# Four blocks of a small transformer: the 31-tap convolution as matmuls, attention's reciprocals as small ones, and layer 0's inverse directly behind its matrices

## The chip, the cores and the metric

The kernel runs on one core of a Trainium2 chip. The core has five engines with queues of their own: TensorE (PE) for matmuls, VectorE (DVE), ScalarE (ACT), GpSimd (POOL), and SyncE (SP), which issues most of the DMAs. PE reads its operands from SBUF and writes into PSUM, eight banks of 128x512 floats; DVE and ACT read the banks. The metric is the device time of one execution in microseconds (us), the median of several runs.

## The reference

The input is a sequence of 256 tokens of 1024 features with a context of as many. `reference` runs two blocks of one kind (layers 0 and 1) and then two of another (the second blocks). Layer 0:

```python
def even_mixer(u_lat, u_ctx, need_ctx, w_in, w_out, conv_w, a_log, dt_bias, out_norm,
               q_norm, w_q_up, kv_norm, w_kv_up, rope):
...
    o_lat, o_ctx = gdn_bidirectional(gdn_prepare(lat[0], lat[2], lat[3], conv_w, a_log, dt_bias),
                                     gdn_prepare(ctx[0], ctx[2], ctx[3], conv_w, a_log, dt_bias))
...
    b_lat = blocked_attention(q_l, jnp.concatenate([k_c, k_l], 1), jnp.concatenate([v_c, v_l], 1), scale)
    y_lat = jnp.concatenate([a_lat, b_lat.reshape(b, s_len, -1)], -1) @ w_out
```

`gdn_bidirectional` is a gated delta rule in chunks of 64 tokens, forwards and backwards. Per chunk and head it builds a lower triangular matrix from the keys, inverts it, and uses the inverse in a scan over the chunks; q, k and v come through a convolution of 5 taps and a silu, q and k also through a norm. Layer 1 has a neighbourhood attention (8 heads) and a grouped one (8 heads on 2 key heads). The two second blocks have an attention in which each token sees the 64 keys that a small index network picks, a pooling, and a causal convolution of 31 taps, each of 256 channels with taps of its own:

```python
def conformer_conv(u, conv_dw, conv_b, ln_g, ln_b, conv_pw):
    a, g = jnp.split(u, 2, axis=-1)
    y = a * jax.nn.sigmoid(g)
    y = lax.conv_general_dilated(
        y, conv_dw[:, None, :], window_strides=(1,), padding=[(CONV_KERNEL - 1, 0)],
        dimension_numbers=('NWC', 'WIO', 'NWC'), feature_group_count=CONV_WIDTH)
    y = y + conv_b
    y = jax.nn.silu(layernorm(y, ln_g, ln_b))
    return jnp.einsum('bsc,cd->bsd', y, conv_pw)
```

Each mixer ends in a linear of its output, and each block in a feed-forward network. Every number is a 32-bit float.

## The kernel before

**Linears.** A weight is loaded from memory in pieces (`wraw`) and split into a high part, cast on ACT (L270, `whi`), and a low part, a subtraction mostly on DVE (L272, `wlo`). Three matmuls (L549 to L551) then stand for one. L306 and L307 split activations in the same way. A matmul of plain floats, such as a transposition (with the identity `const_id`), is one instruction of the program and two in the trace.

**The order of the work.** The source gives each engine its instructions in the order of the calls; a scheduler that runs when the kernel is built then moves them within what their data and buffers allow. So the order on an engine is fixed before the run, and an instruction that waits holds up all that stand behind it on that engine. Buffers set much of it. PSUM banks are handed out by kind (`bank(K, "tp")`), each kind with a number of banks: in layer 0 `g` 3, `s` 2, `tp`, `po`, `gv` one each (`acc` is `s`, `aux` is `g`); in the mixers of layer 1 and of the second blocks `acc` 2, `s` 2, `tp` 2, `aux` and `po` one each (`gv` is `aux`).

**Layer 0** (`l0_mixer`). `gdn_conv` does, for the key, query and value columns, the linear (in `s`) and then the 5 taps: ACT multiplies the identity by a tap, which gives a diagonal 128x128 matrix (L882), and PE multiplies the shifted input by it and sums in a bank (L886). `gdn_norm` normalizes (L941 to L945). `gdn_matrices` transposes (L1028) and forms the products of keys with keys and of queries with keys (L1040), the second kind in its second call; `gdn_blocks` sends the triangular matrices out to memory and back in another layout; `gdn_invert` inverts blocks of 32 on DVE (31 steps of L1086 and L1088), sends them out and back again (`scx`), and finishes on DVE (L1105) and PE (L1115, L1128). `gdn_run` is the scan (from L1154), followed by latent attention (`l0_mla`), four pairs of heads. In the source, the inverse's call comes after the query and value convolutions, the gate's linear and the second matrices. The modulation of layer 0 (`mod_chunk`) multiplies two columns by a weight of 1024x512 for each of its chunks (L372), and brings the rows to columns (L378 for the two gate chunks 4 and 5).

**Attention** (`attend` in layers 0 and 1, `s_attend` in the second blocks). For two heads the scores come in two banks; DVE finds the maximum, ACT takes the exponential and its sum (`sm`), PE transposes the result (L674, L1653), ACT and DVE copy it, and PE multiplies it by the values into `po` (L685, L1659). The sums: DVE takes the reciprocal of a sum that it reads 64 times over (L693), a matmul with the identity turns it (L695) into a bank `rb`, and `attended` multiplies the output by it. In layer 1, `na` is the neighbourhood's attention for a block of 128 tokens, `gqa` the grouped one, and the list `late` holds transposes of the grouped one's keys and queries (L1345).

**The second blocks' mixer** (`s_mixer`). It runs the index network and `choose`, which picks keys on DVE (L1605 to L1621), linears, rotations (`qkv`), and then

```python
        qkv()
        conv(1)
        conv(0)
        choose(0)
        pool_out(0)
        pool_out(1)
        finish()
        att(1)
        att(0)
```

`conv` multiplies the shifted input by a tap on ACT (L1516) and adds it on POOL (L1517), 30 times for each half of the channels. `finish` transposes the sum (L1531), and does the layer norm, the silu (L1543 on) and the product with the pointwise weight (L1553).

## Time and profile before

| | |
|---|---|
| three runs, us | 2169.08, 2181.03, 2183.77 (median 2181.03) |
| the profiled execution, us | 2178.34 |
| its span from first to last instruction, us | 2176.6 |
| its mean granted PE clock | 0.917 |
| PE, DVE, ACT, POOL busy, us | 1992.6, 1382.2, 931.8, 370.7 |

The granted clock is the share of PE's full speed that the chip gave it in a stretch. The times of the rows are of the profiled execution, counted from its first instruction.

### The profile page before, as it was taken

The numbers are of one execution on the slowest core, as the hardware profiler recorded it, in microseconds if no ns is written. First come the engines' busy times: TensorE is split into PE (matmuls) and PEld (weight loads), VectorE is DVE, ScalarE is ACT, GpSimd is POOL, SyncE is SP. The second block draws the span as 40 slices with busy tenths as digits, with TensorE's granted clock in tenths as the row PEclk, the third lists the DMA queues.
The fourth block names the chain that finished last, engine by engine and source line by source line (L and its number), as shares of the span: only waits on it lengthen the run. The fifth ranks groups of instructions, "written<-read, shape, count | busy, mean of one in ns | idle before, by whom it ended". The sixth has DMA issues, their size and how long they took to land.

```text
span 2176.6 us, 30043 instructions
## 1 busy us (share of the span) xinstructions
PE 1992.6 (92%) x11008; PEld 1585.0 (73%) x11008; DVE 1382.2 (64%) x2699; ACT 931.8 (43%) x1612; POOL 370.7 (17%) x454
## 2 busy tenths in 40 slices
PE   6989799898999999899879998988899998879998
PEld 4778578678878778676557887865688787558886
DVE  5665557767776744638575555785765568666644
ACT  4533443344222234444454443753554357345532
POOL 2211112301000000213130002641200057040000
PEclk9999799899999999999788999966999999579999
DMA  8344540233676632223044573513556443055652
GB/s 279 90 112 122 190 131 26 67 98 111 191 259 215 189 106 93 90 68 97 20 145 141 164 230 100 145 54 113 168 175 195 153 113 109 29 164 166 191 186 68
DMA packets 186947, 291.82 MB, mean 134 GB/s; under 512 B 28472, under 2 KB 75704, under 8 KB 186800
## 3 DMA queue, kind: packets, MB, share of 16 engines
q1 hardware_dynamic: 172720, 272.54, 40.2%
q0 software_dynamic: 5472, 16.13, 2.3%
q10 hardware_dynamic: 8608, 1.23, 0.4%
q8 instruction: 87, 1.43, 0.3%
q14 instruction: 60, 0.49, 0.1%
HBM read 281.44 MB, written 8.41 MB: 133 GB/s over the span
## 4 chain that ended last, share of the span: by engine, by line
PE 75%; DVE 13%; DMA 5%; ACT 4%; issue 2%; POOL 1%; SPq 0%; ACTq 0%; DVEq 0%; POOLq 0%
PE acc L549 17%; PE acc L550 17%; PE acc L551 17%; DVE wlo L272 2%; DMA wraw<-in_w_in_dram 2%; PE s L549 2%; PE s L550 2%; PE s L551 2%; PE po L685 2%; PE tp L886 2%; DMA wraw<-in_w_mod_dram 1%; PE gv L372 1%; ACT whi L270 1%; PE tp L674 1%; PE s L1642 1%
## 5 line engine op out<-in xcount | busy, mean ns | idle before, releaser
L272 DVE TENSOR_TENSOR wlo<-wraw,whi 128x512 fp32r<-128x512 f32 (+4 forms) x748 | 488.7, 697 | 292.4 <-ACT whi L270 276.5
L270 ACT CAST whi<-wraw 128x1024 fp32r<-128x1024 f32 (+4 forms) x420 | 413.4, 989 | 456.1 <-PE acc L551 180.9
L549 PE MATMUL acc<-whi,u 128*128 128x512 f32 (+3 forms) x1320 | 512.5, 391 | 28.3 <-ACT u L306 15.9
L550 PE MATMUL acc<-wlo,u 128*128 128x512 f32 (+3 forms) x1320 | 511.7, 389 | 4.4 <-DVE wlo L272 4.4
L551 PE MATMUL acc<-whi,u 128*128 128x512 f32 (+3 forms) x1320 | 510.3, 388 | 0.8 <-DVE u L307 0.7
L549 PEld LDWEIGHTS acc<-whi,u 128*128 128x128 f32 x1320 | 254.3, 193 | 80.9 <-ACT u L306 18.2
L550 PEld LDWEIGHTS acc<-wlo,u 128*128 128x128 f32 x1320 | 254.3, 193 | 55.2 <-DVE wlo L272 8.0
L551 PEld LDWEIGHTS acc<-whi,u 128*128 128x128 f32 x1320 | 253.2, 192 | 52.3 <-DVE u L307 4.3
L272 POOL TENSOR_TENSOR wlo<-wraw,whi 128x512 fp32r<-128x512 f32 (+1 forms) x92 | 115.1, 1280 | 400.5 <-ACT whi L270 400.4
L549 PE MATMUL acc<-u,whi 128*128 128x512 f32 (+1 forms) x480 | 174.1, 369 | 5.0 <-ACT u L1558 2.7
L550 PE MATMUL acc<-u,whi 128*128 128x512 f32 (+1 forms) x480 | 174.0, 364 | 2.4 <-DVE u L307 2.4
L551 PE MATMUL acc<-u,wlo 128*128 128x512 f32 (+1 forms) x480 | 173.1, 365 | 2.2 <-DVE wlo L272 2.2
L1517 POOL TENSOR_TENSOR u<-u,cvm 128x256 f32<-128x256 f32 x120 | 100.3, 836 | 64.2 <-ACT cvm L1516 55.8
L549 PEld LDWEIGHTS acc<-u,whi 128*128 128x128 f32 x480 | 93.9, 197 | 21.6 <-ACT u L1558 3.1
L431 DVE SCALAR_TENSOR_TENSOR msum<-mraw,u,msum 128x512 f32<-128x512 f32 x140 | 100.8, 746 | 13.4 <-DMA mraw<-in_w_mod_dram 12.4
L550 PEld LDWEIGHTS acc<-u,whi 128*128 128x128 f32 x480 | 94.5, 197 | 17.7 <-DVE u L307 3.1
L551 PEld LDWEIGHTS acc<-u,wlo 128*128 128x128 f32 x480 | 94.1, 197 | 17.6 <-DVE wlo L272 2.8
L307 DVE TENSOR_TENSOR u<-aux,u 128x512 fp32r<-128x512 f32 (+2 forms) x92 | 56.8, 629 | 34.8 <-ACT u L306 34.4
L306 ACT CAST u<-aux 128x512 fp32r<-128x512 f32 (+2 forms) x92 | 48.5, 541 | 59.2 <-PE aux L724 25.9
L549 PE MATMUL acc<-whi,dxh 128*128 128x512 f32 x176 | 69.7, 396 | 1.9 <-ACT dxh L306 1.9
L550 PE MATMUL acc<-wlo,dxh 128*128 128x512 f32 x176 | 69.6, 395 | 0.0
L551 PE MATMUL acc<-whi,dxl 128*128 128x512 f32 x176 | 69.0, 396 | 0.0
(501 smaller groups left out, 3037.8 us busy)
## 6 DMA issues: line engine op xcount, KB each, us to landing
wraw<-in_w_up_dram SPq DMA_DIRECT2D x64, 512.0 KB, 3.9
wraw<-in_w_down_dram SPq DMA_DIRECT2D x64, 512.0 KB, 4.2
...
```

The source lines that it names most:

```text
L270: self.K.nc.scalar.copy(hi, raw)
L272: e.tensor_tensor(lo[:, k], raw[:, k], hi.bitcast(F32)[:, k], op=ALU.subtract)
L306: (hi_eng or nc.scalar.copy)(hi, src)
L307: nc.vector.tensor_tensor(lo, src, hi.bitcast(F32), op=ALU.subtract)
L372: nc.tensor.matmul(ps[32 * j:32 * j + 32, :], K.cl[:, g + k, :], raw[:, k, :], start=(g + k < 4), stop=(g + k >= 4))
L431: nc.vector.scalar_tensor_tensor(accs[s], raw[:, k, :], c, accs[s], op0=ALU.mult, op1=ALU.add)
L549: mm(ps, ah, bh, start=start, stop=False)
L550: mm(ps, ah, bl, start=False, stop=False)
L551: mm(ps, al, bh, start=False, stop=stop)
L685: nc.tensor.matmul(po[hh * 64:hh * 64 + 64, c:c + 128], v(hh, j), pts[hh][0][:, j * 128:(j + 1) * 128], start=(j == 0), stop=(j == nj - 1))
L886: nc.tensor.matmul(tp[:, t * 128:(t + 1) * 128], x[:, t // 2, t % 2 * 128 + j:t % 2 * 128 + j + 128], dg[j], start=(j == 0), stop=(j == 4))
L1517: nc.gpsimd.tensor_tensor(o, o, m, op=ALU.add)
```

## The change

1. The second blocks' convolution goes to PE. `taps` makes a diagonal matrix per tap on ACT, and one of the bias as a 32nd tap on an input of ones; `conv` sums 2 x 32 products for each half of the tokens in a bank, `po` for one and `tp` for the other. The result stands by tokens, so that L1531's transposes go. `finish` reads the banks.
2. The sums' reciprocal is taken once, of 2 (or 4) columns, into a tile `R`; at a block's end `normed` spreads it over 512 columns (a copy on DVE), turns it with four matmuls (L700 of the new file) into `aux` (in layer 0 `gv`), and multiplies.
3. The two heads of a pair take score banks of one kind: in layer 1, odd pairs of the grouped attention and of the second block of `na` take `acc`, even ones `s`; in the second blocks head group 1 takes `acc`. Layer 1's `late` runs before `na(1)`.
4. In layer 0 `gdn_invert` is called directly behind `gdn_blocks`, and the query's norm and matrices ahead of the value's convolution and the gate. The second matrices' products go to the banks `gv` and `po` instead of two of kind `g`. Modulation chunks 6 to 9 come before the latent attention, and the gate chunks 4 and 5 within it, before its third pair, with the bias in a tile of its own.

```diff
@@ attend @@
-    sums_row(K, sm.unsqueeze(1), rb, c)
+    nc.vector.reciprocal(R[:, x], sm)
+    c = 128 * x
...
+def inverse_sums(K):
+    return cut(K, [128, 4, 2], F32, "rs", 2)
+
+def normed(K, y, po, R, kind):
+
+    rb = bank(K, kind)
+    w = cut(K, [128, 512], F32, "pt", K.np)
+    K.nc.vector.tensor_copy(w.rearrange("p (x d) -> p x d", d=64), bc(R.rearrange("p x h -> p (x h)"), [128, 8, 64], 2))
+    for x in range(4):
+        K.nc.tensor.matmul(rb[:, x * 128:x * 128 + 128], w[:, x * 128:x * 128 + 128], K.ident,
                            start=True, stop=True)
+    K.nc.scalar.copy(y, rb)
+    K.nc.vector.tensor_tensor(y, po, y, op=ALU.mult)
@@ l0_mla @@
+        if pair == 2:
+            gates()
@@ gdn_matrices @@
-        kk = [aux(K), aux(K)]
+        kk = [bank(K, "gv"), bank(K, "po")] if second else [aux(K), aux(K)]
@@ layer 1 @@
-                   ("s", "acc", "tp", "acc") if t == 1 and pair >= 1 else ("s", "s", "tp", "tp"))
+                   ("acc", "acc", "tp", "tp") if t == 1 and pair % 2 else ("s", "s", "tp", "tp"))
...
-    na(1)
     for f in late:
         f()
+    na(1)
@@ s_conv @@
-    def conv(c):
-        o = cv[:, c, :]
-        nc.scalar.activation(o, yp[:, c, 0:256], AF.Identity, scale=dw[:, i, c, 0:1], bias=dwb[:, i, c:c + 1])
-        na = 31 if c == 0 else 31
-        for j in range(1, na):
-            m = cut(K, [128, 256], F32, "cvm", 2)
-            nc.scalar.mul(m, yp[:, c, j:j + 256], dw[:, i, c, j:j + 1])
-            nc.gpsimd.tensor_tensor(o, o, m, op=ALU.add)
...
+    def taps(c):
+
+        for j in range(32):
+            if j % 3 == 0:
+                dg = cut(K, [128, 3, 128], F32, "dg", 2)
+            nc.scalar.mul(dg[:, j % 3, :], K.ident, dw[:, i, c, j:j + 1] if j < 31 else dwb[:, i, c:c + 1])
+            yield j, dg[:, j % 3, :]
+
+    def conv():
+
+        ps = [bank(K, "po"), bank(K, "tp")]
+        for c in range(2):
+            for j, dg in taps(c):
+                for t in range(2):
+                    nc.tensor.matmul(ps[t][:, c * 128:c * 128 + 128],
+                                     yp[:, c, t * 128 + j:t * 128 + j + 128] if j < 31 else ones, dg,
+                                     start=(j == 0), stop=(j == 31))
+        return ps
@@ s_attend @@
-    pss = [bank(K, "s") for _ in range(2)]
+    pss = [bank(K, "acc" if g else "s") for _ in range(2)]
@@ s_mixer @@
-        conv(1)
-        conv(0)
+        cv = conv()
         choose(0)
         pool_out(0)
         pool_out(1)
-        finish()
+        finish(cv)
@@ l0_mixer @@
-                        LX = gdn_blocks(K, Om)
+                        gdn_invert(K, *gdn_blocks(K, Om))
                     with Pool(K, "gq"):
                         with On(K, pg):
                             gdn_conv(K, W, 0, 4, True, True)
+                        gdn_norm(K, 0)
+                        gdn_matrices(K, True)
+                        with On(K, pg):
                             gdn_conv(K, W, 8, 4, False, True)
                             gdn_gate(K, W)
-                        gdn_norm(K, 0)
-                        gdn_matrices(K, True)
...
-                with On(K, g2):
-                    gdn_invert(K, *LX)
...
-                        for n in range(4, 10):
-                            mod_chunk(K, W, K.po, 0, n)
-                        l0_mla(K, Om)
+                        for n in range(6, 10):
+                            mod_chunk(K, W, K.cur, 0, n)
+                        l0_mla(K, Om, lambda: [mod_chunk(K, W, K.cur, 0, n) for n in (4, 5)])
```

PE in layer 0, before: behind the gate's last linear matmul come the second matrices (keys `u_138`, queries `u_137`) and the inverse.

```order
L886 MATMUL tp_1544<-cvo_1537,u_439 128x128 x4
L886 MATMUL tp_1544<-cdg_1538,u_439 128x128
...
L551 MATMUL s_1692<-whi_1590,u_149 128x512
L1028 MATMUL tp_1755<-const_id_75,u_138 128x128 x4
L378 MATMUL gv_3235<-mrow_3233,const_id_75 2x512
L1028 MATMUL tp_1762<-const_id_75,u_137 128x128 x4
L1040 MATMUL g_1769<-gT_1767,gT_1760 64x64
...
L1115 MATMUL g_2013<-b_2009,u_144 32x32 x32
L1128 MATMUL g_2083<-u_144,b_2010 32x32 x32
```

The same in the new order (L892 is L886 before, L1034 is L1028, L1046 is L1040, L1121 is L1115, L1134 is L1128, L1160 is L1154): the second matrices and the inverse stand directly behind the linear of the values' last chunk (`s_2083`), and ahead of the values' products and of the gate.

```order
L551 MATMUL s_2083<-u_148,wlo_1907 128x512
L1034 MATMUL tp_1715<-const_id_75,u_137 128x128 x4
L1046 MATMUL gv_1722<-gT_1720,gT_1713 64x64
L1046 MATMUL po_1723<-gT_1720,gT_1713 64x64
...
L1121 MATMUL g_1136<-b_1132,u_144 32x32
L1134 MATMUL g_1206<-u_144,b_1133 32x32 x32
...
L1046 MATMUL po_1855<-gT_1852,gT_1845 64x64
L892 MATMUL tp_1945<-cvo_1938,u_436 128x128 x4
L892 MATMUL tp_1945<-cdg_1939,u_436 128x128
...
L1160 MATMUL g_2313<-u_139,u_143 64x64
```

Behind it the values' products and the gate's linear alternate, and the scan's first matmuls (L1160) stand among the gate's.

PE in the first second-block mixer, in the new order: the last wide linear matmul (`acc_12546`), then the taps (L1533) among the index network's products (`s_12829`) and the transposes of queries and keys (L1351, before L1345).

```order
L551 MATMUL acc_12546<-whi_12514,u_9658 128x384
L1533 MATMUL tp_12613<-dg_12624,u_11691 128x128
L1533 MATMUL po_12612<-dg_12624,u_11691 128x128
L1533 MATMUL tp_12613<-dg_12624,u_11691 128x128
...
L1533 MATMUL tp_12613<-dg_12634,u_11691 128x128
L549 MATMUL s_12829<-u_12035,u_12064 128x128
...
L1351 MATMUL aux_12588<-const_id_75,akd_12578 128x128 x2
L549 MATMUL s_12840<-u_12035,u_12071 128x128
L1533 MATMUL po_12612<-dg_12644,u_11691 128x128
```

Of the layer's 128 taps 11 stand ahead of these rows. Its last ones, the transposes of the layer norm (L1552, before L1543), attention's products with the values (L1668, before L1659) and the scores behind them (L1647):

```order
L1533 MATMUL po_12612<-dg_12821,u_11696 128x128
L1533 MATMUL tp_12613<-dg_12821,u_11696 128x128
L1552 MATMUL acc_12953<-const_id_75,lnx_12975 128x128 x2
L1668 MATMUL po_13003<-pt_13027,u_11685 64x256
L1668 MATMUL po_13003<-pt_13039,u_11685 64x256
...
L1647 LDWEIGHTS u_11656
L1647 MATMUL acc_13054<-u_11689,u_11656 128x256
```

The product into `po_13003` stands behind the last tap, since there is one bank `po`.

## Rows read from the trace of the kernel before

**Rows 1.** The page of the kernel before, its parts 1, 4 and 5: busy time of each engine (PEld is PE's weight loads) with its share of the span and its instructions, the shares of the chain of waits by engine, and the group of the convolution's adds (both layers, busy us and mean ns of one).

```profile
PE 1992.6 (92%) x11008; PEld 1585.0 (73%) x11008; DVE 1382.2 (64%) x2699; ACT 931.8 (43%) x1612; POOL 370.7 (17%) x454
...
PE 75%; DVE 13%; DMA 5%; ACT 4%; issue 2%; POOL 1%; SPq 0%; ACTq 0%; DVEq 0%; POOLq 0%
...
L1517 POOL TENSOR_TENSOR u<-u,cvm 128x256 f32<-128x256 f32 x120 | 100.3, 836 | 64.2 <-ACT cvm L1516 55.8
```

**Rows 2.** The windows by stage. Columns: from and to, length, then busy us and instructions of PE, of its weight loads, of DVE, ACT and POOL, then the granted clock of PE (1.00 is full), the busy share of the DMA engines and GB/s.

```profile
204.00:276.00 72.00, 58.93 (x885) 41.81 (x883) 33.79 (x113) 29.28 (x62) 13.11 (x30) 0.75 0.51 170
276.00:384.00 108.00, 105.02 (x1139) 82.09 (x1139) 71.96 (x125) 43.08 (x100) 21.58 (x30) 1.00 0.26 79
1018.00:1138.00 120.00, 98.30 (x537) 67.60 (x537) 79.55 (x148) 53.51 (x106) 30.82 (x30) 0.81 0.23 71
1342.00:1436.00 94.00, 78.29 (x490) 72.26 (x489) 71.91 (x136) 64.70 (x135) 60.93 (x76) 0.94 0.46 130
1436.00:1502.50 66.50, 54.63 (x200) 34.97 (x200) 41.87 (x122) 22.16 (x65) 5.80 (x8) 0.50 0.09 28
1851.00:1919.00 68.00, 55.02 (x201) 35.20 (x201) 43.61 (x124) 21.19 (x64) 5.67 (x8) 0.50 0.09 27
```

**Rows 3.** Three lines of the kernel in the view of one line by shape, all calls of the span: min, median and max ns of one, first and last start. L1516 is the convolution's multiplication, L882 makes a diagonal matrix for layer 0's short convolution, L693 is the reciprocal of the sums.

```profile
L1516 ACT ACTIVATE cvm<-u,u x120: 494/507/550, 1363.5 to 1860.1; 128x256 f32<-128x256 f32 x120
...
L882 ACT ACTIVATE cvo<-const_id,u x32: 385/388/403, 88.9 to 183.6; 128x128 f32<-128x128 f32 x32
...
L693 DVE RECIPROCAL rs<-sm x32: 935/953/954, 311.9 to 1099.8; 128x128 f32<-128x128 f32 x32
L693 DVE RECIPROCAL rs<-asm x8: 1695/1743/1753, 1456.9 to 1908.6; 128x256 f32<-128x256 f32 x8
```

**Rows 4.** PE's time line in layer 0, from the products of the short convolution (L886) to the first linear matmul behind them: start, us, instruction, count.

```profile
137.99 1.91 PE L886 MATMUL tp<-cvo,u 128*128 128x128 f32 x8
139.70 0.64 PE L886 MATMUL tp<-cdg,u 128*128 128x128 f32 x2
...
141.40 1.06 PE L886 MATMUL tp<-cvo,u 128*128 128x128 f32 x8
...
148.12 1.05 PE L886 MATMUL tp<-cvo,u 128*128 128x128 f32 x8
...
152.50 0.47 PE L549 MATMUL s<-u,whi 128*128 128x512 f32 x1
```

**Rows 5.** The windows of two stretches of 6 us around the end of the first second-block mixer's linear work; columns as in rows 2.

```profile
1430.00:1436.00 6.00, 1.98 (x18) 1.58 (x16) 5.83 (x16) 3.88 (x9) 4.56 (x6) 0.84 0.00 1
1460.00:1466.00 6.00, 6.00 (x23) 3.64 (x22) 3.07 (x11) 0.91 (x4) 0.00 (x0) 0.50 0.00 0
```

**Rows 6.** DVE's subtraction that makes the low part of a weight (L272): in 1342–1436 us at 128x384 (from the groups of DVE by shape), and on the page over the whole span, mostly at 128x512.

```profile
L272 DVE TENSOR_TENSOR wlo<-wraw,whi 128x384 fp32r<-128x384 f32 x16 | 12.7, 852 | 0.7 <-ACT whi L270 0.7
...
L272 DVE TENSOR_TENSOR wlo<-wraw,whi 128x512 fp32r<-128x512 f32 (+4 forms) x748 | 488.7, 697 | 292.4 <-ACT whi L270 276.5
```

**Rows 7.** Two pieces of the chain of waits in the first second-block mixer: start, us, what.

```profile
1428.40 0.96 DVE u L1605
...
1490.51 3.38 DVE rs L693 x2
```

**Rows 8.** DVE's time line in layer 0: the first and the last step of the inverse's loop, the norm's multiplication, and the first step that uses what came back from memory. In brackets the idle time before, and what ended it.

```profile
142.94 0.27 DVE L1086 TENSOR_TENSOR b<-gL,u 128x62 f32<-128x62 f32 x1 [13.65 <-DMA gL<-scr]
...
186.03 2.99 DVE L945 TENSOR_TENSOR u<-u,rsy 128x512 f32<-128x512 f32 x2
...
191.43 0.22 DVE L1088 TENSOR_TENSOR u<-u,b 128x62 f32<-128x62 f32 x1
...
199.56 1.23 DVE L1105 STREAM_TRANSPOSE b<-u 32x1024 f32<-32x1024 f32 x1 [3.29 <-DMA u<-scx]
```

**Rows 9.** PE's time line in layer 0: a chunk of linear work behind the last query product and the next product; then a wait for a modulation weight, the first matmuls of the inverse on PE and the first of the scan.

```profile
162.56 0.48 PE L549 MATMUL s<-u,whi 128*128 128x512 f32 x1
...
168.25 1.05 PE L886 MATMUL tp<-cvo,u 128*128 128x128 f32 x8
...
232.80 1.92 PE L372 MATMUL gv<-wraw,u 128*32 128x512 f32 x4 [4.63 <-DMA wraw<-in_w_mod_dram]
...
240.02 1.20 PE L1115 MATMUL g<-b,u 32*32 32x32 f32 x64
...
262.33 0.33 PE L1154 MATMUL g<-u,u 64*64 64x64 f32 x2 [0.27 <-ACT u L1132]
```

**Rows 10.** The windows of the last part of layer 0's stretch ahead of the scan, and of the scan's first operands; columns as in rows 2.

```profile
246.00:262.00 16.00, 15.46 (x402) 9.98 (x394) 14.44 (x67) 9.83 (x26) 5.33 (x21) 0.57 0.64 207
262.00:276.00 14.00, 13.36 (x117) 11.72 (x114) 7.65 (x24) 5.73 (x12) 0.00 (x0) 0.55 0.25 87
```

**Rows 11.** Layer 1's attention: two windows, columns as in rows 2, and of PE's time line the first and the last of the five lone transposes there that follow a wait.

```profile
1024.00:1048.00 24.00, 19.54 (x103) 12.97 (x103) 19.05 (x49) 11.24 (x25) 9.98 (x12) 0.72 0.11 36
1048.00:1078.00 30.00, 23.78 (x97) 14.61 (x96) 12.70 (x21) 9.37 (x22) 0.00 (x0) 0.60 0.07 20
...
1050.24 0.44 PE L1345 MATMUL aux<-const_id,lkd 128*128 128x128 f32 x2 [0.53 <-ACT pt L713]
...
1056.37 1.09 PE L1345 MATMUL aux<-const_id,lx 128*128 128x128 f32 x4 [1.01 <-DVE u L307]
```

74 lines of the change are left out of this document (29 added, 45 removed).

## The prediction

> **What bounds the kernel now.** I read the page first, then the windows by stage, then TensorE's (PE's) time line where a window shows idle time or a low clock, and the chain of waits for the two places where the chain leaves PE. The page shows PE busy for 92% of the span, and 75% of the chain on it [rows 1]. So a change pays in only two ways: it fills time in which PE idles, or it brings PE's granted clock back to its upper level (1.00 is 2.4 GHz, 0.50 is 1.2 GHz). The windows show where either is to be had [rows 2]. In 204–276 us (layer 0, between the V convolution and the scan) PE idles 13 of 72 us at a mean clock of 0.75; in 1018–1138 (layer 1's attention) 22 of 120 at 0.81; in 1436–1502.5 (the end of the first second-block mixer) 12 of 66.5 at 0.50, and the same again in 1851–1919. In 276–384 the clock is 1.00 and 105 of 108 us are busy: there nothing is to be had. The change touches just the stretches with slack; outside them I expect no difference.
>
> The sum is made against the profiled execution, 2178.3 us. It lies 2.7 us under the median of the three runs, 2181.0, whose own spread is 15 us. The bound of 1% used for the chances is 22 us: faster is below 2159, slower above 2203.
>
> **1. The convolution of the two second-block mixers.** What goes is 120 adds on GpSimd (POOL), 0.836 us each, 100.3 us [rows 1], with their 120 ScalarE (ACT) multiplications of 0.507 us. What comes, per layer, is 64 diagonal matrices on ACT (31 taps and the bias, two channel halves) and 128 matmuls on PE, which the trace counts as 256, since each full-float one is two instructions. Layer 0's short convolution has the same two operations. ACT makes a 128x128 diagonal in 0.388 us [rows 3], so 24.8 us a layer in place of 60 x 0.507 = 30.4. On PE, 40 instructions take from 148.12 to 152.50 = 4.38 us at the upper clock, 0.110 each; at the lower, eight take 1.71 us (137.99 to 139.70), 0.214 each [rows 4]. So a layer's convolution costs PE **28.0 us at 2.4 GHz and 54.7 us at 1.2 GHz**.
>
> Does that fit into what PE leaves idle? In the order of the change only 11 of the 128 matmuls come early. The rest stand after the last wide linear matmul, between the query and key transposes and the scores, where before PE waits for VectorE (DVE). That linear work ends at about 1432 us: in 1430–1436 PE is busy 2.0 of 6 us at a clock of 0.84, and from there on it is 0.50, even in 1460–1466, where PE is busy all the time [rows 5]. From 1436 to the end PE does 54.6 us of work at 0.50 [rows 2], that is 27 us at 1.00 if all of it scales; I take 30. With the convolution in the gap I expect the clock to stay up: eight of its kind take 1.91 us at 137.99 and 1.06 at 141.40, so it rises within a run of them, and at 148.12 it is up [rows 4]. Then 28 + 30 = 58 us of PE work follow.
>
> The start moves too. While POOL adds, DVE's steps are long: L272 on 128x384 takes 852 ns, more than the 697 ns mean of a group that is mostly 128x512 [rows 6]; by elements it should take 0.52. That is 5 us on these 16 alone, and DVE is on the chain there (1428.40) [rows 7]. Of perhaps 10 us that DVE gets back, I take half for the linear work's end, 1427, since not each of these steps has PE waiting behind it. The Trainium skill (SBUF — State Buffer, "SBUF: two separate sides") says that DVE and GpSimd share a port pair as an exclusive lock, where a DVE step with two SBUF inputs blocks for the whole GpSimd instruction. The trace agrees in kind, with 0.33 us per L272 step, less than half an add. By that rule up to half of a layer's 50 us of adds, 25 us, would come back to DVE.
>
> To 1427 + 58 = 1485 I add 12 us of waits: ACT's diagonals, of which few buffers are open, and the end, where the layer norm waits for the last tap and attention's products wait for the banks that the convolution holds. Before, PE waits about as much from 1436 on. The end is then near 1497 against 1502.5, **5.5 us a layer, 11 in both**. The bounds: all 12 us of waits hidden and 10 us from DVE, 22 a layer; clock at 0.50 throughout, 1427 + 54.7 + 54.6 + 12 = 1548, a loss of 46 a layer.
>
> **2. The sums' reciprocals.** 32 reciprocals of 0.953 us and 8 of 1.743 go, 44.4 us of DVE [rows 3]. 40 on 2 or 4 columns come, which I price by DVE's shortest kind of row, 0.22 us [rows 8], 8.8 in all, and 12 copies of 128x512 (0.70 by [rows 6]), 8.4. DVE loses 27 us, but almost nowhere on the chain, where PE covers it. In the mixers' ends two of 1.74 stand on the chain, 3.38 us at 1490.51 [rows 7]; I have put that in the 12 us above. Elsewhere: 0, hidden by PE; uncovered, 0.95 per score pair.
>
> **3. Layer 0.** DVE's triangular inverse already runs at 142.94–191.65 [rows 8], and its read-back from memory comes at 199.56. So it isn't DVE's loop that moves but PE's use of it: PE multiplies by it only from 240.02, after a 4.63 us wait for a modulation weight [rows 9]. In the new order, PE does the query products, the V linear and then at once the second matrices and the inverse; V's products and the gate linear come after. Query products end at 162.56; two more V chunks of 5.69 us each (162.56 to 168.25) [rows 9] bring PE to 174. There it waits for the norm, whose multiplication ran at 186.03–189.0 behind two V steps of 0.7 us that now come later: until about 187, **13 us of new idle time**. About 5 us of transposes and products fit in until the inverse's read-back, about 2 us earlier than before at 198: 6 us more. From 240.02 to 262.33 the inverse took 22 us, with some 5 us of modulation work, and at a clock near 0.57 [rows 9, 10]; I take 15, so 213. Then come four V products of 4.38 and 96 gate matmuls, four chunks of 5.69, together 40 us, and, mixed into them, the scan's first operands, which took 262–276 at 0.55, 13.4 us busy or 7.4 at the upper clock [rows 10]. With 5 us of hand-offs this reaches at about 266 what before was reached at 276: 10 us. The modulation's chunks leave this stretch, for the scan and, the two gate chunks, for behind two pairs of attention: some 3 us of PE work at the upper clock, paid there. Their eight weight loads pass, on SP's queue, behind those of the scan and of the first heads, their bias loads on POOL's; both are early enough to cost nothing, and if not, 4.63 us each [rows 9]. **Net 7 us.** The bounds: 20 if the new waits shrink, -25 if the 47 us run at half clock for half of their length.
>
> **4. Layer 1.** The transposes of the doubled keys and of the last queries stand alone on PE at 1050–1058, with waits before them of 0.5 to 1.0 us each, some 5 us in all. The clock is 0.72 in 1024–1048 and 0.60 in 1048–1078, 43.3 us busy [rows 11]: at 1.00 some 15 us less. Moved between the pairs of the second neighbourhood block they fill its waits, and heads in unlike banks (two "s", then two "acc") let the next pair's scores start. I take the 5 us of waits and a fifth of the clock's 15: **8 us**; bounds 0 and 20.
>
> Sum: 11 + 7 + 8 = 26, so 2152 us; the median's 2.7 us are left out as smaller than its spread.
>
> **The rivals.**
> *The freed engines are more of the bound than I take them for* (0.22). If DVE gets back nearer 20 us a layer than 10, the linear work ends earlier and the waits between taps are filled: 15 a layer, 14 in layer 0, 14 in layer 1, 58 in all, **2120**. For it: DVE is busy 71.9 of 94 us in 1342–1436 [rows 2] and on the chain. Against it: PE's own work sets those stretches once the taps are in.
> *PE takes what POOL gave for nothing* (0.22). The clock stays up through the taps but drops behind them, in the waits of layer norm and attention: the last 17 us of PE work take 34. The mixers then lose 11 a layer, 22, against 15 from the other parts: **2185**, no change. For it: the mixer's end is made of short matmuls that wait for ACT and DVE in turn, and now it stands at 0.50 with PE busy 82% [rows 2].
> *The convolution runs at the lower clock* (0.13), slower. If PE has to wait for ACT's diagonals or for the weights every few taps, the clock doesn't come back: 54.7 and 54.6 us, 46 a layer, 92 less 15: **2255**; with the lower clock for half of the time, 2205. The point from which it decides is a mean granted clock of 0.7 between the last linear matmul and the mixer's end. For it: 1460–1466 stays at 0.50 without a gap [rows 5]. Against it: the taps at 141.40 and 148.12 [rows 4]. The Trainium skill (TensorE: Matmul & The Clock Gate, "What's actually happening") has the throttled state as the default, which activity releases; by it layer 0's 13 us wait would also cost the clock, and the -25 of part 3 stands for that.
>
> My forecast has 0.43, with a range of its own of 2138 to 2170. Below 2159 lie the first rival and three quarters of the forecast: 0.55. Above 2203 lie the third rival and a little of the second: 0.17. Within 1%: 0.28. The range 2112 to 2205 leaves out the far end of the first rival (0.07) and most of the third (0.12).
>
> **What would show it.** Part 1: 512 new PE instructions of 0.11 us; POOL under 280 us busy; a granted clock over 0.8 from 1432 to the mixer's end, and that stretch no longer than 70 us. At 0.5 the third rival holds. Part 2: DVE down by some 25 us. Part 3: PE idle near 174–187 and again before 198, the scan dense by 267. Part 4: no lone transposes and a clock over 0.9. It would be wrong if the attention's products wait long for the banks of the taps, since the scores behind them on PE wait too.

## The result, and the profile after

The changed kernel takes **2194.46 us** (median of 8 runs, 2187.16 to 2200.57) against 2170.26 (8 runs, 2166.74 to 2183.77) for the kernel before on the same chip: a ratio of **1.0091, 95% interval 1.0066 to 1.0117**. It is slower by 0.9%, clear of the noise though within the bound of 1%, where 2152 us and a gain were forecast. Its profiled execution takes 2197.15 us with a span of 2195.4, against 2178.3 and 2176.6 before.

The page of the changed kernel, the lines that answer to [rows 1] and to the second of [rows 6]:

```profile
PE 2015.3 (92%) x11512; PEld 1621.0 (74%) x11512; DVE 1319.5 (60%) x2711; ACT 919.3 (42%) x1616; POOL 272.6 (12%) x336
...
PE 81%; DVE 9%; ACT 4%; DMA 4%; issue 2%; ACTq 0%; POOL 0%; SPq 0%; DVEq 0%; POOLq 0%
...
L272 DVE TENSOR_TENSOR wlo<-wraw,whi 128x512 fp32r<-128x512 f32 (+4 forms) x748 | 466.9, 667 | 298.2 <-ACT whi L270 282.3
```

The work did move as the diff says: POOL lost 98 us, DVE 63 us, and the whole kernel is longer all the same. Less of the chain lies on DVE (9% for 13%) and more on PE (81% for 75%). So the loss is where PE runs slowly or waits. I set marks at DVE's first step of the norm behind each mixer's and each feed-forward network's output linear (L532). A mixer's leg runs from the last group of marks of the network ahead of it to its own first mark:

```
us                                    before  changed
to layer 0's mixer end                 464.2    480.2
layer 1's mixer                        229.1    229.2
first second-block mixer               207.0    207.1
second second-block mixer              216.8    212.3
networks between them, and the end    1059.5   1066.7
```

Sixteen of the 19 us of the profiled executions are lost before 480 us, and layer 1, where 8 us were to be gained, gains nothing. The second blocks' mixers gain 4.4 us, not 11. The last row is code that no edit touches, and it differs by 7 us. Such legs differ between other kernels too: layer 1's mixer takes 228.2 us in e3 and 237.2 in e9 (at a clock of 0.83), the first second-block mixer 199.6 us in e7 and 207.0 before, none of them touched by the edit. So one leg of one kernel doesn't show less than about 9 us; only legs that agree over several kernels do.

Layer 0, PE's time line of the changed kernel, from the wait for the norm to the first state product of the scan (start, us, instruction; in brackets the idle time and its releaser):

```profile
185.68 1.09 PE L1034 MATMUL tp<-const_id,u 128*128 128x128 f32 x4 [11.15 <-DVE u L951]
...
191.31 1.08 PE L1034 MATMUL tp<-const_id,u 128*128 128x128 f32 x4 [1.70 <-ACT gT L1036]
...
197.73 0.37 PE L1046 MATMUL gv<-gT,gT 64*64 64x64 f32 x1 [5.33 <-ACT gT L1036]
...
199.84 0.36 PE L1121 MATMUL g<-b,u 32*32 32x32 f32 x3
...
224.37 2.07 PE L892 MATMUL tp<-cvo,u 128*128 128x128 f32 x8
...
274.17 1.13 PE L1201 MATMUL g<-gu,gkd 64*128 64x128 f32 x8 [0.88 <-ACT gu L1167]
```

The windows over it, columns as in [rows 2]:

```profile
174.00:200.00 26.00, 7.15 (x86) 5.00 (x85) 18.34 (x45) 3.75 (x5) 4.62 (x4) 0.59 0.65 149
200.00:224.00 24.00, 20.66 (x580) 18.39 (x583) 6.04 (x11) 11.66 (x20) 0.00 (x0) 0.50 0.45 112
224.00:264.00 40.00, 38.09 (x313) 32.38 (x308) 8.05 (x14) 9.71 (x24) 0.72 (x1) 0.97 0.26 87
264.00:300.00 36.00, 29.95 (x227) 24.23 (x225) 22.10 (x93) 13.02 (x35) 12.33 (x29) 0.76 0.32 106
```

PE does 7 us of work in 26, then the inverse and the rest of the second matrices at a clock of 0.50. The linear work that used to stand here comes after both.

The first state product came at 267.4 us before, so 7 of the 16 us are lost ahead of it. The other 9 are lost behind it: from there to the mark of layer 0 it is 206.0 us for 196.8. In 284 to 304 the clock falls a second time, before and changed:

```profile
284.00:304.00 20.00, 19.84 (x208) 14.48 (x202) 9.55 (x17) 8.43 (x19) 2.26 (x3) 1.00 0.38 118
```

```profile
284.00:304.00 20.00, 17.32 (x111) 13.48 (x112) 16.48 (x78) 5.16 (x10) 2.26 (x3) 0.59 0.40 129
```

The middle of the first second-block mixer's end in windows of 12 us, and of PE's time line the step behind the last tap (which starts at 1481.81 and takes 0.39 us):

```profile
1454.00:1466.00 12.00, 12.00 (x106) 10.36 (x105) 6.48 (x24) 7.77 (x23) 0.00 (x0) 1.00 0.14 44
1466.00:1478.00 12.00, 11.75 (x96) 10.38 (x94) 5.12 (x21) 8.54 (x26) 0.00 (x0) 1.00 0.01 2
1478.00:1490.00 12.00, 8.40 (x51) 5.97 (x50) 4.45 (x18) 1.51 (x5) 0.00 (x0) 0.83 0.00 1
1490.00:1502.00 12.00, 11.24 (x37) 6.96 (x37) 4.77 (x12) 3.52 (x12) 0.00 (x0) 0.50 0.15 44
```

```profile
1485.79 0.53 PE L1552 MATMUL acc<-const_id,lnx 128*128 128x128 f32 x2 [3.60 <-DVE lnx L1549]
```

PE is full at 1.00 as long as the taps last. Then it waits 3.6 us for the layer norm, and attention's products behind it run at 0.50.

The whole end of a second-block mixer, from its last wide linear matmul to its output linear, is in the kernel before, first and second mixer:

```profile
1430.90:1502.50 71.60, 55.70 (x212) 35.90 (x212) 46.83 (x135) 25.14 (x73) 9.56 (x13) 0.52 0.09 26
1848.20:1918.90 70.70, 56.05 (x212) 36.09 (x212) 46.33 (x129) 22.92 (x69) 8.07 (x12) 0.52 0.08 25
```

and in the changed kernel, with the part of the first one behind the last tap as a third row:

```profile
1440.60:1521.50 80.90, 71.34 (x450) 54.70 (x448) 36.27 (x121) 37.30 (x117) 1.15 (x2) 0.82 0.10 30
1858.30:1935.50 77.20, 67.72 (x451) 52.52 (x449) 36.15 (x122) 36.28 (x116) 1.14 (x2) 0.87 0.10 32
1482.20:1521.50 39.30, 30.00 (x100) 17.55 (x100) 14.69 (x41) 10.62 (x37) 1.15 (x2) 0.64 0.11 35
```

The linear work ends earlier, counted from the mark ahead of the mixer: after 114.3 us for 122.2 in the first mixer and 123.6 for 134.2 in the second. The end behind it is longer by 9.3 and 6.5 us, and that takes back all of the gain in the first mixer and more than half of it in the second.

In layer 1 the changed kernel has a wait that the one before has not. The line view of the copy that spreads the reciprocals (L698, in `normed`), and of the matmuls that turn them (L700), over the span; the indented rows say what the engine had waited for:

```profile
L698 DVE COPY pt<-rs x12: 408/422/428, 375.2 to 1930.8; 128x512 f32<-128x512 f32 x12
...
  PE po L686: 3.1, 3
```

```profile
L700 PE MATMUL aux<-const_id,pt x64: 275/275/582, 1045.6 to 1932.2; 128*128 128x128 f32 x64
...
  DVE pt L698: 18.5, 16
```

The copy takes a `pt` tile. There are two of them, and the softmax of each head takes one: the copy has to wait until attention's products (L686) are done with theirs, PE waits for the copy, and by the buffers the next head's `pt` is not free until PE has read it. L718 in `attended` takes one of the two `p` tiles as well and holds it until the block is split; before, one `pt` tile served there (L712), for a copy and a product.

### The profile page after: what moved, and what is told of

It reads as the page before. It is cut to its first block, busy times and chain, and to the rows that moved or that the text cites. A ratio compares the mean times of both kernels' runs of the same rounds, so it can differ in the third digit from the quotient of the medians.

```text
span 2195.4 us, 30851 instructions
## 1 busy us (share of the span) xinstructions
PE 2015.3 (92%) x11512; PEld 1621.0 (74%) x11512; DVE 1319.5 (60%) x2711; ACT 919.3 (42%) x1616; POOL 272.6 (12%) x336
## 3 DMA queue, kind: packets, MB, share of 16 engines
q1 hardware_dynamic: 172720, 272.54, 40.4%
## 4 chain that ended last, share of the span: by engine, by line
PE 81%; DVE 9%; ACT 4%; DMA 4%; issue 2%; ACTq 0%; POOL 0%; SPq 0%; DVEq 0%; POOLq 0%
PE acc L549 18%; PE acc L551 18%; PE acc L550 18%; PE s L549 2%; PE s L550 2%; PE s L551 2%; PE tp L892 2%; PE gv L372 1%; PE po L686 1%; PE po L1533 1%; DMA wraw<-in_w_mod_dram 1%; PE tp L674 1%; PE tp L1533 1%; DVE wlo L272 1%; PE aux L729 1%
## 5 line engine op out<-in xcount | busy, mean ns | idle before, releaser
L272 DVE TENSOR_TENSOR wlo<-wraw,whi 128x512 fp32r<-128x512 f32 (+4 forms) x748 | 466.9, 667 | 298.2 <-ACT whi L270 282.3
L272 POOL TENSOR_TENSOR wlo<-wraw,whi 128x512 fp32r<-128x512 f32 (+1 forms) x92 | 114.5, 1274 | 410.1 <-ACT whi L270 409.9
L532 DVE TENSOR_TENSOR y<-acc,u 128x512 f32<-128x512 f32 x40 | 27.4, 687 | 57.7 <-ACT yj L531 57.7
```

The costliest lines, as they stand in the source:

```text
L272: e.tensor_tensor(lo[:, k], raw[:, k], hi.bitcast(F32)[:, k], op=ALU.subtract)
L532: nc.vector.tensor_tensor(y[:, cs], ps, G(t)[:, cs], op=ALU.mult)
```

## The experiments

Each ratio is to runs of the kernel before on the same chip, with its 95% interval; a difference in us is that of the two medians. Where a kernel reorders much, the marks above are used too.

### Which part loses

**e1**: the changed kernel with layer 0 and the modulation in the old order.

```diff
-                        gdn_invert(K, *gdn_blocks(K, Om))
+                        LX = gdn_blocks(K, Om)
...
-                        gdn_norm(K, 0)
-                        gdn_matrices(K, True)
-                        with On(K, pg):
                             gdn_conv(K, W, 8, 4, False, True)
                             gdn_gate(K, W)
+                        gdn_norm(K, 0)
+                        gdn_matrices(K, True)
...
+                    gdn_invert(K, *LX)
```

> The changed kernel with layer 0 in its old order (inverse called behind the second matrices, these behind the values' convolution and the gate, their products in banks of kind g, all six modulation chunks ahead of the latent attention); convolution and attention as changed. Theory A, that layer 0's order is the whole loss (its landmark, the last step of the output linear, came 16 us later in the changed kernel: 480.2 against 464.2): 3 to 6 us below the kernel before, ratio 0.997 to 0.9985. Theory B, that each part costs some of it and layer 0 only moves it about: above the kernel before by 5 us or more.

Measured: 2172.1 us, 0.9989 [0.9970, 1.0007]. That is 2.4 us below, a little short of A's 3 to 6 but not clear of it; B falls. The rest of the change, priced at -19, brings 2.4 us. Layer 0's mark comes at 459.6 us, so 20.6 of the 22 us between this kernel and the changed one lie ahead of it.

**e2**: only layer 0's new order, in the kernel before (the same lines the other way round, with the banks `gv` and `po` and the modulation's new places).

```diff
-                        LX = gdn_blocks(K, Om)
+                        gdn_invert(K, *gdn_blocks(K, Om))
...
-                            mod_chunk(K, W, K.po, 0, n)
-                        l0_mla(K, Om)
+                            mod_chunk(K, W, K.cur, 0, n)
+                        l0_mla(K, Om, lambda: [mod_chunk(K, W, K.cur, 0, n) for n in (4, 5)])
```

> The kernel before with layer 0's new order alone. Theory A: 16 to 20 us slower than before (ratio 1.007 to 1.009), with PE idle for about 11 us before 186 us and the clock at 0.5 in 200 to 224, as in the changed kernel. Theory B: below 10 us.

Measured: 2197.9 us, 1.0103 [1.0079, 1.0128], 23 us more than before, and so a little over A's 16 to 20. PE is busy 7.9 of 26 us in 174 to 200, and the clock is 0.50 in 200 to 224, as A had it. From e1 to the changed kernel the same step costs 22 us. So the loss belongs to layer 0's order, with or without the other parts.

**e3**: only the convolution on PE.

```diff
-        conv(1)
-        conv(0)
+        cv = conv()
```

> The kernel before with the convolution on TensorE alone. Theory A: -6 to +2 us against before, since in the changed kernel one mixer lost 1.4 us and the other won 4.2. Theory B: 5 to 10 us slower, the 56 us of taps not being hidden where the attention stands in its old form.

Measured: 2163.6 us, 0.9961 [0.9934, 0.9988], that is -11 us by the medians (2174.5 before) and -8 by the ratio, near the 11 of the prediction's first term and a little past A's -6. Its linear work ends 8.1 and 10.4 us earlier than before, and the ends behind it are about as long as before (71.3 and 73.4 us).

**e4**: only the sums' reciprocals, the banks of one kind and `late` ahead of `na(1)`.

```diff
-    sums_row(K, sm.unsqueeze(1), rb, c)
+    nc.vector.reciprocal(R[:, x], sm)
...
-    pss = [bank(K, "s") for _ in range(2)]
+    pss = [bank(K, "acc" if g else "s") for _ in range(2)]
```

> The kernel before with the attention's part alone (reciprocals of 2 and 4 columns, the sums turned once, banks of one kind for two heads, layer 1's late transposes first). Theory A: within 3 us of before, as layer 1's attention lay within 1 us of it in the changed kernel. Theory B: 3 to 8 us slower, from the chain of copy, four matmuls and multiplication at each block's end.

Measured: 2155.8 us, 0.9911 [0.9886, 0.9935], -19 us: neither theory's number. By the marks the gain lies in the second blocks' mixers (196.1 and 207.6 us), not in layer 1's (227.4). e3 and e4 together would be -30; e1, which holds both, has -2.4, and its second blocks' mixers take 207.4 and 213.6 us. Something that each can do alone is lost when both stand in one kernel. It is lost behind the last tap of the first mixer, in e3 and in e1:

```profile
1464.40:1491.90 27.50, 17.27 (x88) 10.33 (x88) 14.73 (x36) 8.46 (x27) 1.14 (x2) 0.90 0.09 23
```

```profile
1454.90:1495.30 40.40, 31.26 (x102) 18.45 (x101) 14.77 (x42) 10.66 (x37) 1.14 (x2) 0.59 0.12 38
```

PE's idle time there is not longer in e1 (9.1 us) than in e3 (10.2); its work, 102 matmuls for 88, takes 31.3 us for 17.3, at the lower clock.

**e8**: only the modulation chunks' new places.

```diff
-                        for n in range(4, 10):
-                            mod_chunk(K, W, K.po, 0, n)
...
+                        for n in range(6, 10):
+                            mod_chunk(K, W, K.cur, 0, n)
...
```

> The kernel before with the order of the modulation chunks alone changed (6 to 9 first, 4 and 5 before the third pair of heads). Theory A: -5 to +2 us, since the wait for the bias leaves the stretch before the scan. Rival: 5 us or more slower, if the gate chunks' weights are late in the attention.

Measured: 2169.8 us, 0.9981 [0.9955, 1.0006]. They cost nothing, as the prediction had it.

### Layer 0

**e6**: in the kernel before, only the inverse directly behind its matrices.

```diff
-                        LX = gdn_blocks(K, Om)
+                        gdn_invert(K, *gdn_blocks(K, Om))
...
-                with On(K, g2):
-                    gdn_invert(K, *LX)
```

> The kernel before with the inverse called directly behind its matrices, nothing else of layer 0 moved; the values' products and the gate still stand on PE ahead of it. Theory A (the loss is PE standing behind the query's norm, since the second matrices come ahead of the values' products): within 4 us of before. Theory E (the inverse's reading back from memory is what PE waits for): 10 us or more slower.

Measured: 2192.3 us, 1.0112 [1.0080, 1.0145], +20 us where A had 4 at most. E's time holds, but not for E's reason: PE has no long wait for what comes back from memory. Its inverse stands at 202 to 222 us. Its longest waits ahead of the scan, on PE's time line of e6:

```profile
249.08 1.70 PE L372 MATMUL gv<-wraw,u 128*32 128x512 f32 x4 [3.79 <-DMA wraw<-in_w_mod_dram]
...
261.03 1.94 PE L372 MATMUL gv<-wraw,u 128*32 128x512 f32 x8 [3.90 <-DVE mrow L381]
...
269.83 1.92 PE L372 MATMUL gv<-wraw,u 128*32 128x512 f32 x4 [2.01 <-DMA wraw<-in_w_mod_dram]
```

These are the modulation's waits. One of 4.63 us stands in the kernel before too [rows 9], and the inverse's matmuls stood among them. But from 174 us to the first state product PE idles 15.0 us here and 13.1 before, and that product comes at 265.8 us, 1.7 earlier than before. The 11.1 us by which layer 0's mark is later are lost behind it. The windows there, before and e6:

```profile
276.00:306.00 30.00, 29.04 (x301) 19.73 (x301) 15.27 (x26) 11.83 (x25) 5.74 (x8) 0.98 0.45 135
```

```profile
276.00:306.00 30.00, 28.85 (x273) 22.14 (x274) 16.07 (x47) 10.62 (x19) 4.55 (x6) 0.76 0.45 141
```

**e7**: only the norm and the second matrices ahead of V's convolution and the gate (banks `gv` and `po`); the inverse's call stays late.

```diff
-                            gdn_conv(K, W, 8, 4, False, True)
-                            gdn_gate(K, W)
                         gdn_norm(K, 0)
                         gdn_matrices(K, True)
+                        with On(K, pg):
+                            gdn_conv(K, W, 8, 4, False, True)
+                            gdn_gate(K, W)
```

> The kernel before with the query's norm and the second matrices called ahead of the values' convolution and the gate (their products in gv and po), and the inverse called late. Theory A: 8 to 20 us slower, PE idle for about 11 us at 174 to 186. Theory E: within 4 us.

Measured: 2189.5 us, 1.0083 [1.0051, 1.0114], +17 us: A holds. The scheduler puts the inverse's first matmul at 205.2 us all the same (240.0 before), so this edit too moves the inverse on PE. The wait for the norm is there as in the changed kernel:

```profile
188.86 1.09 PE L1028 MATMUL tp<-const_id,u 128*128 128x128 f32 x4 [11.02 <-DVE u L945]
```

**e9**: the norm and the second matrices between V's convolution and the gate.

```diff
                             gdn_conv(K, W, 8, 4, False, True)
-                            gdn_gate(K, W)
                         gdn_norm(K, 0)
                         gdn_matrices(K, True)
+                        with On(K, pg):
+                            gdn_gate(K, W)
```

> The kernel before with the query's norm and the second matrices called behind the values' convolution but ahead of the gate (their products in gv and po; the inverse called late, as before). Theory A (PE stands behind the query's norm, for which the values' products were the cover): no wait of 11 us before the query's transposes, and at least 8 us of the 14 us that the matrices alone cost layer 0 come back: its landmark, the first step of the output linear's end, at most at 470 us (464.2 before, 478.4 with the matrices ahead of the values). Theory F (any splitting of the gate's linear from the values costs as much, since the inverse and the matrices then stand without other work to mix with): 474 or later.

Measured: 2165.9 us, 0.9963 [0.9930, 0.9996], layer 0's mark at 453.5 us (464.2 before). A's 470 holds, F falls. The window, and the same transposes with no wait ahead of them:

```profile
174.00:206.00 32.00, 31.11 (x280) 27.49 (x279) 19.56 (x41) 10.60 (x19) 2.99 (x3) 1.00 0.57 116
```

```profile
206.80 0.60 PE L1028 MATMUL tp<-const_id,u 128*128 128x128 f32 x4
```

The norm is DVE's: its multiplication starts at 184.33 us here and at 184.00 in the changed kernel. With V's products and the gate's linear beside it (the scheduler puts the linear there, from 181 us on) PE is busy for 31.1 of 32 us at 1.00; without them 7.2 of 26 at 0.59. They are the cover, and the change takes just them away. The inverse's first matmul comes at 197.4 us here: it is early, as the change wanted it, and the wait is gone.

The same kernels by the first state product of the scan, and the rest of layer 0 behind it; the last row counts the modulation's matmuls (L372) ahead of that product, as the trace counts them, of 160:

```
us                        before  changed    e2     e6     e7     e9
first state product        267.4   274.2   278.6  265.8  271.6  239.2
from there to the mark     196.8   206.0   213.0  209.6  206.8  214.2
modulation ahead of it       112      80      80    104     80     72
```

Wherever PE does the inverse early, the rest is longer, by 9 to 17 us. Part of that is modulation that is left for it: four such matmuls take 1.05 us at the upper clock, so 32 are about 8 us. Part is the clock (e6, and the changed kernel in 284 to 304). The shares are not separated. Nor is the split between e6's and e7's edits: over the kernel they lose 20 and 17 us and e2, which holds both, 23; by layer 0's mark 11.1, 14.1 and 27.4.

### Attention and the sums

**e5**: e1 with the second groups' scores back in `s`.

```diff
-    pss = [bank(K, "acc" if g else "s") for _ in range(2)]
+    pss = [bank(K, "s") for _ in range(2)]
```

> The changed kernel with layer 0 in its old order and, in the second blocks' attention, both head groups' scores in the banks s, as before. Theory C, that the scores of the second group, sent to the banks acc, can't stand among the taps (finish holds one of acc's two banks) and so leave PE idle for 3.6 us behind the last tap, the clock falling to 0.5: the clock stays above 0.8 to the mixer's end, each mixer's stage 6 to 10 us shorter than with acc, 10 to 20 us in all below the kernel before (ratio 0.990 to 0.995). Theory D, that the banks po and tp held by the taps alone cause that tail: no change against acc, ratio near 0.999.

Measured: 2169.4 us, 0.9991 [0.9968, 1.0014]. C falls with its 10 to 20 us and its clock: as long as the tiles are shared, the banks of the last scores are not the main thing that the mixers' end waits for. Behind the last tap of the first mixer it is 34.0 us for e1's 40.4, but the last tap comes later. The clock there still drops from 0.91 to 0.53 once the taps are over:

```profile
1455.00:1475.00 20.00, 14.81 (x85) 10.32 (x84) 9.10 (x29) 4.04 (x12) 0.00 (x0) 0.91 0.08 27
1475.00:1495.00 20.00, 15.58 (x50) 9.25 (x48) 4.80 (x11) 5.79 (x23) 1.14 (x2) 0.53 0.08 26
```

**e10**: in the kernel before, only the sums' reciprocals.

```diff
+    w = cut(K, [128, 512], F32, "pt", K.np)
...
+    y = cut(K, [128, 512], F32, "p", K.np)
+    normed(K, y, po, R, "aux")
```

> The kernel before with the small reciprocals alone, banks and the order of layer 1 as before. The attention's part as a whole won 19 us. Theory G, that the win is DVE's time and the shorter chain of the sums in the second mixers: at least 12 of the 19. Theory H, that it is the banks of one kind for two heads: below 6.

Measured: 2193.9 us, 1.0105 [1.0067, 1.0143]: +19 us by an edit that takes DVE work away. Neither theory had that. Its profiled execution took 4722 us, so no trace of it is read, and where the loss arises is not shown by e10 itself.

**e11**: e5 with tiles of their own for `normed` and `attended`.

```diff
-    w = cut(K, [128, 512], F32, "pt", K.np)
+    w = cut(K, [128, 512], F32, "nw", 1)
...
-    y = cut(K, [128, 512], F32, "p", K.np)
+    y = cut(K, [128, 512], F32, "ny", 1)
```

> As the kernel with the old layer 0 and banks s for both head groups, but with tiles of their own for the two tiles of the sums' last step, which otherwise take a buffer p and a buffer pt of the softmax (two each). Theory I, that these buffers hold back the softmax of the next 128 tokens, whose scores came only 1476 us, behind the sums' matmuls: 8 to 16 us below that kernel, ratio to before 0.993 or less. Theory J, that the banks po and tp held by the taps set the tail: no change, 0.999.

Measured: 2131.5 us, 0.9819 [0.9777, 0.9861]. **Two tiles of their own are worth 38 us** against e5. J falls. I holds in kind, with more than twice its 8 to 16 us, and most of it not where I looked: layer 1's mixer takes 203.7 us for 228.0, the second blocks' mixers 196.1 and 206.0 for 204.4 and 213.1. Behind the last tap of the first of them:

```profile
1439.60:1463.10 23.50, 15.37 (x81) 9.61 (x80) 11.79 (x36) 8.14 (x25) 1.14 (x2) 0.85 0.10 27
```

**e12**: e11 with the taps summed in banks `acc` and the result's transposes in `aux`.

```diff
-        ps = [bank(K, "po"), bank(K, "tp")]
+        ps = [acc(K), acc(K)]
...
-        back = acc(K)
+        back = aux(K)
```

> As the one with tiles of their own, and the taps sum in the two banks acc, which no linear needs then, the layer norm's transposes in aux; so po and tp are free for attention, and its products with the values can stand among the taps. Theory J: no wait of PE behind the last tap over 2 us with a clock that falls to 0.5, and 10 to 20 us below the kernel before (0.991 to 0.995). Theory I alone: as the one with tiles of their own, within 3 us.

Measured: 2145.5 us, 0.9876 [0.9830, 0.9921], 14 us slower than e11, although attention's products now stand among the taps. Neither theory had a loss. By the marks some 6 us of it lie in layer 0, which this edit does not touch, and 5.8 in the first second-block mixer (201.9 us for 196.1). That the products wait for the banks of the taps, which the prediction feared, was at least not what held the mixers up.

**e13**: the whole changed kernel with the two tiles of their own (the edit of e11).

```diff
+    w = cut(K, [128, 512], F32, "nw", 1)
...
+    y = cut(K, [128, 512], F32, "ny", 1)
```

> The changed kernel whole, with tiles of their own for the sums' last step and nothing else. Theory K, that the change loses two things, some 20 us by layer 0's order and some 35 us of what it could win by those two buffers: it lies 10 to 25 us below the kernel before (ratio 0.989 to 0.995), with layer 1's mixer (from the first block's end at the feed-forward network to its own) at 212 us or less in place of 229, and layer 0 as slow as in the changed kernel. Theory L, that the buffers matter only with the second group's banks s: within 5 us of the changed kernel, 1.006 or more.

Measured: 2151.9 us, 0.9881 [0.9817, 0.9945]: K holds, with 24 us below before and layer 1's mixer at 203.7; layer 0's mark comes at 475.3. The total lies on the forecast of 2152 by chance: layer 0's mark is still 14 us later than e11's, and the rest gains more than forecast. Layer 1's mixer as one window, in the kernel before, the changed one, and e13, and then the largest of PE's waits within layer 1's attention in the changed kernel (us in total, times, longest):

```profile
888.40:1117.50 229.10, 200.94 (x1061) 148.88 (x1060) 144.32 (x354) 102.53 (x203) 41.17 (x55) 0.88 0.23 73
```

```profile
904.70:1133.90 229.20, 199.17 (x1058) 148.40 (x1058) 135.30 (x358) 102.15 (x203) 41.21 (x55) 0.89 0.23 73
```

```profile
898.00:1102.00 204.00, 184.74 (x1059) 140.20 (x1058) 130.75 (x358) 101.90 (x203) 40.87 (x55) 0.96 0.26 82
```

```profile
PE aux L700 <- DVE pt L698: 6.7, 4, 3.8
PE tp L674 <- ACT p L671: 4.1, 3, 1.4
```

With the same instructions, own tiles take 10.8 us from PE's idle time (30.0 to 19.3, each the length less the busy time) and 14.4 from its busy time, because the clock goes from 0.89 to 0.96 (busy time times clock is 177 us in both). PE's order in layer 1 differs between the two kernels as well, since the scheduler orders within what the buffers allow; how much of the 25 us is the wait at the tiles and how much the order is not separated. The row on L700 is gone from e13's waits there; the line view of the copy shows what it waits for now, over the whole span:

```profile
L698 DVE COPY nw<-rs x12: 408/426/429, 355.2 to 1882.6; 128x512 f32<-128x512 f32 x12
...
  PE aux L700: 0.6, 1
```

e13 also has the banks of one kind for the second blocks' head groups, and e11 has not. Behind the last tap e13's two mixers take 34.5 and 31.1 us, e11's 23.5 and 23.9. Over the whole mixers the difference is 6.0 and 1.3 us, within what untouched legs vary, so whether those banks cost something beside the taps stays open.

**e15** and **e16** take part 2 and the banks apart: e15 is e10 with the tiles of their own, e16 only the banks of one kind and `late` first.

```diff
-    w = cut(K, [128, 512], F32, "pt", K.np)
+    w = cut(K, [128, 512], F32, "nw", 1)
...
-    y = cut(K, [128, 512], F32, "p", K.np)
+    y = cut(K, [128, 512], F32, "ny", 1)
```

> The kernel before with the small reciprocals alone, now with tiles of their own. Theory K: the 20 us that the small reciprocals lost with the softmax's buffers go, ratio 0.990 to 1.000. Theory M, that the loss comes from the four matmuls and the copy at the block's end: still above 1.006.

Measured: 2166.1 us, 0.9948 [0.9909, 0.9988]. K holds, M falls: the same reciprocals that cost 19 us with shared tiles gain 10 with their own.

```diff
-                   ("s", "acc", "tp", "acc") if t == 1 and pair >= 1 else ("s", "s", "tp", "tp"))
+                   ("acc", "acc", "tp", "tp") if t == 1 and pair % 2 else ("s", "s", "tp", "tp"))
...
-    na(1)
     for f in late:
         f()
+    na(1)
```

> The kernel before with the banks of one kind and layer 1's order of late transposes alone, reciprocals as before. Theory K: 8 to 20 us below before, mostly in layer 1's mixer (215 us or less in place of 229), where my prediction looked for 8. Theory N, that these banks win only with the small reciprocals, since the bank of the sums holds back the next block: within 4 us.

Measured: 2162.8 us, 0.9939 [0.9913, 0.9965], -13 us. K's total holds and N falls, but layer 1's mixer takes 224.8 us, not the 215 at most that K had; the second blocks' mixers take 197.2 and 205.4 us for 207.0 and 216.8. Layer 1's mixer, by banks and sums:

```
us                              old banks      banks of one kind
one reciprocal per pair          229.1          224.8 (e16)
one at the end, shared tiles     not read       227.4 (e4), 227.5 (e1), 229.2 (changed)
one at the end, own tiles        224.4 (e15)    203.7 (e11), 203.7 (e13)
```

Both together are worth 23 to 25 us there, and four kernels agree on it (e12 has 203.8, e14 206.5). Each alone has 4 to 5 us, less than untouched legs vary. My reading, which no run isolates, is that only when neither the score banks nor the tiles hold the next pair back can it run into the one before; the shared tiles close one of the two ways.

**e14**: e11 with layer 0 as in e9.

```diff
                             gdn_conv(K, W, 8, 4, False, True)
-                            gdn_gate(K, W)
                         gdn_norm(K, 0)
                         gdn_matrices(K, True)
+                        with On(K, pg):
+                            gdn_gate(K, W)
```

> The kernel with tiles of their own and banks s, with the second matrices behind the values' convolution and ahead of the gate. If the two gains add, 5 to 10 us below the one without: ratio 0.977 to 0.980. If the gain of that order was chance of the schedule, 0.982.

Measured: **2126.3 us, 0.9751 [0.9699, 0.9804]**, 50 us less than before and 68 less than the changed kernel. It is the best version found, though its interval overlaps e11's, and its layer 0 mark is only 1.2 us earlier (460.4 for 461.5): that e9's gain adds to e11's is not shown.

## Why the prediction was wrong

**The sum** was 11 + 0 + 7 + 8 = 26 us of gain. The kernel loses 19 us by the profiled executions, 20 by the ratio, 24 by the medians. The edits' mechanisms were seen in part; two terms failed, and either repaired alone takes the loss away: e1 is level with the kernel before (0.9989), e13 lies 24 us below it.

**Part 3, layer 0, is the first step that failed**: -7 us forecast, +22 measured (e1 to the changed kernel; +23 in e2). The new idle time was seen and sized nearly right: 13 us of waiting for the norm and 6 before the inverse, in the trace 11.15, 1.70 and 5.33. Three things behind it were not.
- "I take 15, so 213" for the inverse: from 199.84 to 224.37 it is 24.5 us, at 0.50. I had divided a stretch of the kernel before, at 0.57, as if the clock would rise. But PE came out of 26 us with 7 of work, and small matmuls did not bring the clock back though PE was busy for 20.7 of 24 us.
- V's products, the gate and the scan's first operands took 224.4 to about 273, 48.5 us, the 47 and a bit that I had. But the gain "at about 266 what before was reached at 276" compared two points of the program that are not the same: the first state product of the scan was at 267.4 before and is at 274.2. Even 266 would have been 1.4 us, not 10.
- Behind the scan's start I had only the modulation's 3 us of PE work. From the first state product to the layer's mark the changed kernel takes 206.0 us for 196.8 (e1 193.0), with 32 modulation matmuls more to do there, some 8 us, and a second fall of the clock, 0.59 in 284 to 304. The modulation's new places alone cost nothing (e8). So the loss there is the new order's as a whole; e6 and e7, with the chunks in their old places, have it too.

The bounds of the term, 20 of gain to 25 of loss, did hold the result; I took the wrong side of them. The nearest row for the clock was the 0.55 to 0.57 of [rows 10], and half the clock was what came.

**Part 2 at "0, hidden by PE"** is the second failure, and the larger. The instructions were counted and the tiles were not. DVE's 27 us did go (28.5 in e15, 63 in all with the convolution's share), but the copy that replaces them takes one of two `pt` tiles and the result one of two `p` tiles, so it stops the softmax that follows. Alone it costs 19 us (e10), with own tiles it gains 10 (e15), and in the changed kernel the tiles cost 43 (e13).

**Part 4 at -8** was right in kind, but not in place. Banks of one kind give -13 over the kernel (e16). By the marks only 4 us of that lie on layer 1's leg, where the 8 were forecast; the second blocks' legs, which I had left out, are 10 and 11 us shorter. The clock of layer 1's mixer could come back to 0.96, as I had forecast "over 0.9". In the changed kernel it stays at 0.89, and with own tiles alone it rises (e13), so part 2 holds it down.

**Part 1 at -11** agrees with e3's -11 for the convolution alone. Taps run at 1.00; POOL is under 280 us (272.6). The wide linear matmuls end 8.1 and 10.4 us earlier in e3, 7.9 and 10.6 in the changed kernel, where I had 5, with some taps among them. The end behind them, forecast at 70 us at most, takes 71.3 and 73.4 us in e3, but 81.0 and 77.2 in the changed kernel, at a clock of 0.82 and 0.87; so there the two mixers together gain 4 us instead of 11.

L272 on 128x384 fell from 852 to 733 ns in the mean, 0.12 us where I had 0.33, although POOL's taps are gone. The time lines of DVE and POOL in the changed kernel show why: six of the 16 steps stand beside POOL's pooling steps and take a microsecond each, the others half of it, near the 0.52 by elements.

```profile
1416.53 5.84 DVE L272 TENSOR_TENSOR wlo<-wraw,whi 128x384 fp32r<-128x384 f32 x6
...
1428.75 1.95 DVE L272 TENSOR_TENSOR wlo<-wraw,whi 128x384 fp32r<-128x384 f32 x4
```

```profile
1418.19 0.94 POOL L1507 TENSOR_TENSOR u<-pls,const_rest 64x256 f32<-64x256 f32 x1
```

The Trainium skill (SBUF — State Buffer, "SBUF: two separate sides") has the port pair that DVE and GpSimd share as an exclusive lock. The trace agrees in kind: a step of about 0.5 us takes 1.0 beside POOL's. My estimate by that rule was up to 25 us a layer, and the linear work ended only 8 to 10.6 us earlier.

**The rivals.** The second, "PE takes what POOL gave for nothing", with 2185 us, came nearest in time, and its mechanism is in the trace: at 1.00 until the last tap, then a wait of 3.60 us, then 0.50, and behind the last tap PE is busy for 30.0 of 39.3 us at 0.64, where the rival had 34. But the linear work's earlier end pays for it: the first mixer's leg is 0.1 us longer and the second's 4.5 shorter, rather than 11 a layer lost. The time came out near 2185 mainly by what layer 0 and the tiles lost, and that is chance. The third rival's point, a mean clock under 0.7 from the last linear matmul to the mixer's end, was not reached (0.82 and 0.87). The first rival's 2120 is near what e14 reaches, but through tiles and cover, not through freed engines. The range, 2112 to 2205, holds the result.

**What stays open**: why e3's and e4's gains (-30 together) shrink to 2 in e1. The place is known: behind the last tap e1's two mixers take 40.4 and 37.3 us, e3's 27.5 and 29.6, and most of the difference is the clock. With the old banks own tiles bring the first from 34.0 (e5) to 23.5 (e11); with the banks of one kind it stays at 34.5 (e13). So the shared tiles are a cause, and the banks may be another; by which wait the clock comes down beside the taps, and not without them (e4), I did not single out. Nor is e12's loss explained, of which a part lies where its edit changes nothing.
